# Three norm boundaries of a two-layer diffusion step: modulation sums in quarters, and three moves around them

## The chip, the cores and the metric

The kernel runs on one core of a Trainium2 chip. The core has a matrix engine (PE, in the profile; PEld is its weight load), a vector engine (DVE), a scalar engine (ACT), a general engine (POOL) and a queue that issues transfers (SP). The metric is the device time of one execution in microseconds; less is better.

## The reference, cut to what matters

Two groups of 128 tokens, a context pass and a denoising step, run through the same two layers with 2048 features. Each layer is a mixer (layer 0: latent attention and grouped attention side by side; layer 1: differential attention) and a gated convolutional FFN. Ahead of each of the four stands a norm with a modulation that comes from a condition vector:

```python
mod = jax.nn.silu(cond) @ w_ada[l] + b_ada[l]
sh1, sc1, gt1, sh2, sc2, gt2 = jnp.split(mod[:, None, :], 6, axis=-1)
h = rmsnorm(x, g_norm_mix[l]) * (1 + sc1) + sh1
...
x = x + gt1 * m
h = rmsnorm(x, g_norm_ffn[l]) * (1 + sc2) + sh2
x = x + gt2 * conv_ffn(h, ...)
```

So a norm needs all of x, a sum of squares over the features, and only then can the next weight product start. `w_ada` alone has 2 x 2048 x 12288 numbers, so its product is as much a matter of memory traffic as the layers are.

## The kernel before, in words

**Layout.** Everything is kept transposed: 128 partitions of features, 16 such chunks (KD = 16), 256 columns (NT: 128 tokens of each group). Float32 values are split into a high part (`wh`, `hx[:, k, :NT]`, a cast on ACT) and a low part (`wl`, `hx[:, k, NT:]`, a subtraction on DVE), and each product is three matmuls of 128 x 256: high-high, high-low, low-high. A weight chunk is 16 blocks of 128 x 128, loaded as one tile of 1 MB (`raw`), split in two halves of 8 blocks.

**Order.** A planner places instructions on each engine by a simulated time line, earlier ones first, so an instruction whose inputs are ready early may be placed ahead of others. `tc.keep_in_program_order(i)` (called `pin`) fixes an instruction behind the one that was traced just before it on its engine. `tc.issue_after(j)` places a block's instructions on j's engine behind j. On the chip each engine then works its own list in that order and waits by semaphores.

**The modulation.** `w_ada` is worked off in units (layer, which of the six vectors, quarter of its features). A unit of `ROWS` is four tiles of 1 MB in two buffers (`araw`). Tile t is summed by `sum_rows` (line 579) with four matmuls that go to four groups of 32 columns of the array, one for each quarter g of the tile; when all four tiles are in, `ada_finish` gives two steps: `copy` (line 523, ACT copies the sum out of PSUM into the tile `am`, of which there is one) and `turn` (line 530, four transposes on PE; then a reduction and an addition on DVE, lines 532 and 540). Most of these run through `row_step`, between the chunks of other products; `later` holds steps that are still to be taken. `ensure` takes steps until a unit is done. One unit is kept back for each boundary and summed inside `modulated`.

**A norm boundary.** There are three that go through `modulated`: A, from the output projection of layer 0's attention to the first FFN; B, from the first FFN to mixer C; C, from mixer C's output projection to the second FFN. At the last chunk (c = 15) of the stage before, `residual` first makes a `Ready`: it loads the next stage's first three weight chunks and splits four of their six halves ((0,0), (0,1), (1,0), (2,0)); the half (0,1) lies in a pool called `extra`. Then the residual is added (line 763, DVE), squared (line 191, ACT) and the squares are summed over the features by one-column matmuls with the running sum (line 229) and the last square (line 230). Then come a small scaling (line 206, DVE), the power -1/2 (line 210, POOL), a diagonal (line 236, DVE) and a matmul that spreads it over the partitions (line 244). In the gaps of this chain PE sums the first tile of the kept unit (ahead of the diagonal) and the second (behind line 244).

`rows_in_turn` then makes the 16 normed rows: for each, x times the spread factor (line 676, DVE), scale and shift for group 0 (line 692, DVE; rows 7 and 11 on ACT, line 690) and for group 1 (line 694, ACT), the cast into hx (line 695, ACT), and one row later the low part (line 679, DVE). Between rows stand the splits of the halves that are still open: `steps` names them by row. `Ready.product` (line 433) multiplies the three chunks with the rows as they come, 144 matmuls in the order `ORDER`, in which the third chunk runs two rows behind and the third modulation tile is summed at the place of `None`. The fourth tile's sum and the copy are handed on as `last_rows`, and the transposes as `turn`; they run in the middle of the next stage's fourth and fifth chunk (`between` in `gemm`).

**What follows the product.** `modulated` ends with `W.ahead(pin)`: the first half of the fourth chunk's weights is split (line 249 ACT, line 250 DVE), pinned. In an FFN stage the first three results go through `conv` with everything pinned: line 1355 (ACT), lines 1358 and 1361 (DVE), then another `W.ahead(pin)`. There are three PSUM banks for results (`acc`), so the fourth chunk's product waits until the first result has been read. In mixer C the first results are rotated and copied (lines 1247 to 1253), unpinned.

**Boundary A** has one thing more. Layer 0's unit (0, 3, 1) is still open when the last chunk of the output projection comes up; `ensure(l, 4)`, `ensure(l, 3)` and the loop over `later` trace its last sums, its copy and its transposes there, ahead of the chunk in the program's order but not pinned against it.

## Time and profile before

| | us |
|---|---|
| median of 3 runs (lowest, highest) | 2308.39 (2308.24, 2310.5) |
| the profiled execution, its own time | 2307.44 |
| its span, first to last instruction | 2305.7 |
| PE busy in the span | 2269.9 (98%) |
| DVE busy | 1824.0 (79%) |
| ACT busy | 1180.7 (51%) |
| HBM traffic | 603.01 MB read, 4.75 MB written |

Times in the trace count from the first instruction. A row of a timeline reads: start, duration, engine, line of the kernel, operation, out<-in, shape, count, and in brackets the idle time of the engine before it and what ended it. Matmuls are pipelined: one of 128 x 256 is listed with 0.28 us, while the next starts 0.11 us later. A row of the windows view reads: from:to, length, then busy time (and instructions) of PE, PEld, DVE, ACT and POOL, the granted clock of PE as a share of full speed, the share of the DMA engines' time, and GB/s.

### The profile page before, as it was taken

To read this page: it belongs to the slowest core of one execution; us is meant where nothing else is said; L and a number is where in the kernel's file an instruction comes from. 1 tells how busy PE (TensorE), PEld (TensorE's weight loads), DVE (VectorE), ACT (ScalarE), POOL (GpSimd) and SP (SyncE) were. 2 spreads that over 40 slices of the span, in tenths; PEclk is the share of its full clock that TensorE was granted. 3 is DMA by queue.
4 is the path that set the end of the run, shared out by engine and by line. 5 is a ranking of instruction groups with operands and counts; after the bars stand their busy time and mean duration, and the time that the engine had idled before them with its cause. 6 is when DMAs were issued, how large, how long until landed. Compare 5 with 4: busy or idle time off the path is not lost. (4 is left out here: it accounts for less than half of the span.)

```text
span 2305.7 us, 47396 instructions
## 1 busy us (share of the span) xinstructions
PE 2269.9 (98%) x19812; PEld 2178.4 (94%) x19812; DVE 1824.0 (79%) x2683; ACT 1180.7 (51%) x1880; POOL 117.4 (5%) x100
## 2 busy tenths in 40 slices
PE   8999999999999999999999999999999999999998
PEld 6888878799999999999989999898999999999997
DVE  5667749789989999999879989787899755666654
ACT  4347654655553455554465555446555434555553
POOL 0001101000000000002200000020000000000011
PEclk9999999999999999999999999999999999999999
DMA  9997789767768767777767787876677555555553
GB/s 390 386 368 276 298 325 393 261 233 263 257 248 311 291 260 272 254 260 273 291 238 271 294 316 288 313 297 236 241 256 262 193 199 188 199 191 193 200 188 125
DMA packets 92565, 610.81 MB, mean 265 GB/s; under 512 B 9984, under 2 KB 17856, under 8 KB 20544
## 3 DMA queue, kind: packets, MB, share of 16 engines
q1 hardware_dynamic: 92352, 607.80, 71.1%
q8 instruction: 155, 2.54, 0.4%
q14 instruction: 58, 0.48, 0.1%
HBM read 603.01 MB, written 4.75 MB: 264 GB/s over the span
## 5 line engine op out<-in xcount | busy, mean ns | idle before, releaser
L249 ACT CAST wh<-raw 128x1024 fp32r<-128x1024 f32 (+1 forms) x772 | 773.5, 1009 | 901.1 <-PE acc L447 685.7
L250 DVE TENSOR_TENSOR wl<-raw,wh 128x1024 fp32r<-128x1024 f32 (+1 forms) x772 | 899.8, 1182 | 286.2 <-ACT wh L249 278.5
L446 PE MATMUL acc<-hx,wh 128*128 128x256 f32 x3440 | 952.8, 277 | 2.3 <-DVE cv L1361 0.8
L450 PE MATMUL acc<-hx,wl 128*128 128x256 f32 x3440 | 951.4, 277 | 0.2 <-DVE wl L250 0.2
L447 PE MATMUL acc<-hx,wh 128*128 128x256 f32 x3440 | 951.5, 277 | 0.0
L446 PEld LDWEIGHTS acc<-hx,wh 128*128 128x128 f32 x3440 | 646.1, 188 | 9.9 <-issue 5.9
L450 PEld LDWEIGHTS acc<-hx,wl 128*128 128x128 f32 x3440 | 645.5, 188 | 6.4 <-issue 2.5
L447 PEld LDWEIGHTS acc<-hx,wh 128*128 128x128 f32 x3440 | 646.1, 188 | 1.0 <-issue 0.8
L556 DVE CUSTOM_DVE_ANT_0 junk<-araw,condb 128x2048 f32<-128x2048 f32 (+1 forms) x192 | 442.8, 2306 | 0.1
L447 PE MATMUL acc<-g,wh 128*128 128x256 f32 x1408 | 388.3, 276 | 0.0
L450 PE MATMUL acc<-g,wl 128*128 128x256 f32 x1408 | 388.0, 276 | 0.0
L446 PE MATMUL acc<-g,wh 128*128 128x256 f32 x1408 | 387.8, 276 | 0.0
L447 PEld LDWEIGHTS acc<-g,wh 128*128 128x128 f32 x1408 | 264.3, 188 | 0.0
L450 PEld LDWEIGHTS acc<-g,wl 128*128 128x128 f32 x1408 | 264.2, 188 | 0.0
L446 PEld LDWEIGHTS acc<-g,wh 128*128 128x128 f32 x1408 | 264.1, 188 | 0.0
L198 POOL TENSOR_TENSOR sqacc<-sqacc,sq 128x256 f32<-128x256 f32 x61 | 83.5, 1368 | 1607.7 <-issue 1250.8
L1013 PE MATMUL acc<-hx,wh 128*128 128x256 f32 x608 | 111.8, 284 | 1.0 <-ACT hx L983 0.6
L1013 PEld LDWEIGHTS acc<-hx,wh 128*128 128x128 f32 x608 | 92.7, 189 | 9.4 <-issue 4.9
L1355 ACT ACTIVATE cv<-acc,convw 128x256 f32<-128x256 f32 x176 | 98.4, 559 | 1.6 <-PE acc L433 1.6
L763 DVE SCALAR_TENSOR_TENSOR x<-acc,mod,x 128x128 f32<-128x128 f32 x192 | 57.9, 343 | 38.4 <-PE acc L450 37.5
L1361 DVE SCALAR_TENSOR_TENSOR cv<-acc,convw,cv 128x254 f32<-128x254 f32 x176 | 84.3, 479 | 3.7
L1013 PE MATMUL acc<-hx,wl 128*128 128x256 f32 x304 | 84.5, 279 | 0.0
(287 smaller groups left out, 2461.7 us busy)
## 6 DMA issues: line engine op xcount, KB each, us to landing
raw<-w_up SPq DMA_DIRECT2D x176, 1024.0 KB, 4.8
araw<-w_ada SPq DMA_DIRECT2D x160, 1024.0 KB, 5.3
raw<-w_down SPq DMA_DIRECT2D x88, 1024.0 KB, 4.8
raw<-w_in_c SPq DMA_DIRECT2D x48, 1024.0 KB, 5.6
raw<-w_in_ab SPq DMA_DIRECT2D x20, 1024.0 KB, 12.4
araw<-w_first SPq DMA_DIRECT2D x16, 1024.0 KB, 8.3
condb<-w_first SPq DMA_DIRECT2D x16, 1024.0 KB, 9.4
raw<-w_out_ab SPq DMA_DIRECT2D x16, 1024.0 KB, 6.9
```

The lines of the kernel that those rows point to most:

```text
L198: pool.tensor_tensor(out=st["acc"], in0=st["acc"], in1=sq, op=ALU.add)
L249: pin(act.copy(out_hi, src))
L250: pin(dve.tensor_tensor(out=out_lo, in0=src, in1=out_hi.bitcast(F32), op=ALU.subtract))
L446: fixed(pe.matmul(ps[:, :n], wh, xh(k), start=(i == 0), stop=False))
L447: fixed(pe.matmul(ps[:, :n], wh, xl(k), start=False, stop=False))
L450: fixed(pe.matmul(ps[:, :n], wl, xh(k), start=False, stop=(i == last)))
L556: tc.keep_in_program_order(dve.tensor_tensor_reduce(out=junk, in0=raw, in1=condb[:, c].rearrange("p (g n) -> p g n", g=4), scale=1.0, scal ...
L763: i = dve.scalar_tensor_tensor(out=x[:, c, s], in0=ps[:, s], scalar=mod[:, l, 3 * which + 2, c, g:g + 1], in1=x[:, c, s], op0=ALU.mult, op ...
L1013: pin(pe.matmul(ps, w, hx[:, k, lo:lo + NT], start=first and k == ks[0] and n == 0, stop=last and k == ks[-1] and n == 2, skip_group_check ...
L1355: pin(act.activation(y, ps, AF.Identity, scale=cw[:, 1, m:m + 1], bias=cw[:, 3, m:m + 1]))
L1361: pin(dve.scalar_tensor_tensor(out=y3[:, :, :T - 1], in0=p3[:, :, 1:], scalar=cw[:, 2, m:m + 1], in1=y3[:, :, :T - 1], op0=ALU.mult, op1=A ...
```

## The change

It has four parts, all at the norm boundaries.

1. *Quarters.* In `modulated` the kept unit's tiles are no longer summed one by one. `fill(n)` takes the next n quarters: three behind the old stage's last matmul, ahead of the statistic's matmuls (two at A); then, behind them, up to the end of tile 1 (at B three); then, behind the spreading matmul, the rest. All are pinned.
2. *Third tile, and third chunk's half, in old memory.* Where `more` is true (A and C, not B), the pool `extra` also takes the half (2,1) of the weights and three quarters of the unit's third tile (`next3`); its fourth quarter goes into the tile `am`. So the third tile's four quarters are summed behind the spreading matmul too, the cast of (2,1) moves from row 8 to the chain (behind that of (1,1)), and its low parts to rows 4 and 9. The product then takes the three chunks in step (`AT_ONCE`), with no sum inside. At B, `ORDER` and its sum stay.
3. *The end of the product.* At all three boundaries the fourth tile's sum is pinned directly behind the product and its copy follows, both ahead of `W.ahead(pin)`; only the transposes are left for the fourth chunk.
4. *Last visit ahead of the last chunk.* At A, unit (0, 3, 1) is summed and copied ahead of the last chunk, whose first matmul is pinned behind it (`held`); its transposes, reduction and addition run at the start of `modulated`, on DVE behind the last residual.

And the first row changes its order: row 1's product on DVE comes behind row 0's scaling, ACT writes row 0 into hx in two parts, and writes group 1 once more into h for the low part.

```diff
+AT_ONCE = [(c, k, part) for k in range(EARLY) for part in ("xl", "x") for c in (0, 1, 2)]
+AT_ONCE += [(c, k, "all") for k in range(EARLY, KD - 2) for c in (0, 1, 2)]
+AT_ONCE += [(c, k, "all") for c, k in ((0, KD - 2), (1, KD - 2), (0, KD - 1), (2, KD - 2), (1, KD - 1), (2, KD - 1))]
...
-        def __init__(self, W, extra):
+        def __init__(self, W, extra, more):
+            self.more = more
+            self.hi, self.lo = {}, {}
+            if more:
+                self.room(2, 1, extra)
+                self.third = T_(extra, [P, 3, 512], "next3", bufs=1)
             self.raws = [W.load() for _ in range(3)]
...
-    def gemm(blocks, xh, xl, n=NT, first=0, between=None):
-        fixed = lambda i: tc.keep_in_program_order(i) if between else i
+    def gemm(blocks, xh, xl, n=NT, first=0, between=None, held=False):
+        fixed = lambda i: tc.keep_in_program_order(i) if between or held else i
...
             fixed(pe.matmul(ps[:, :n], wh, xh(k), start=(i == 0), stop=False))
+            held = False
...
-            if c + 1 < KD:
+            if 0 < c < KD - 1:
                 times(c + 1)
...
+            if c == 0:
+                times(1)
+                pin(act.activation(hx[:, c, T:NT], h[:, T:], AF.Identity, scale=a_(1), bias=b_(1)))
+                pin(act.copy(hx[:, c, :T], h[:, :T]))
             pin(act.activation(h[:, T:], h[:, T:], AF.Identity, scale=a_(1), bias=b_(1)))
-            pin(act.copy(hx[:, c, :NT], h))
             if c:
+                pin(act.copy(hx[:, c, :NT], h))
                 low(c - 1)
...
+        turn = later.pop() if (l, which) == (0, 1) and len(later) == 1 else None
+        if turn:
+            done.add((0, 3, 1))
...
+        if ready.more:
+            parts = ready.third, T_(tmp, [P, 512], "am", bufs=1)
+            for part, g in zip(parts, (slice(0, 3), 3)):
+                sp.dma_start(out=part, in_=A["w_ada"][u[0], u[1], u[2], 2][:, g])
+        groups = [raws[t][:, g] for t in range(2) for g in range(4)]
+        if ready.more:
+            groups += [parts[0][:, 0], parts[0][:, 1], parts[0][:, 2], parts[1]]
         hx = T_(keep, [P, KD, ROW], "hx", F32R)
+        ada["ps"] = bank()
+        at = [0]
+
+        def fill(n):
+            for _ in range(n):
+                t, g = divmod(at[0], 4)
+                pin(pe.matmul(ada["ps"][32 * g:32 * g + 32, :], condw[:, 4 * t + g, :], groups[at[0]],
+                              start=(t == 0), stop=(t == 3), skip_group_check=True))
+                at[0] += 1
+
         tied[0] = True
+        if turn:
+            with tc.issue_after(st["added"]):
+                turn()
+        fill(2 if turn else 3)
         ready.room(1, 1)
         with tc.issue_after(st["squared"]):
             ready.high(1, 1)
+            if ready.more:
+                ready.high(2, 1, pin=pin)
         r = stat_rstd(st, D, att_bank)
-        sum_rows(0, raws[0], bank())
+        fill(8 - at[0] if ready.more else 3)
         dg = diagonal(r, (0, 1))
         ready.low(1, 1, 0, 4, pin)
         rb = spread(dg, bank=att_bank)
-        sum_rows(1, raws[1])
+        fill(len(groups) - at[0])
         tied[0] = False
-        raws += [load_tile(2), load_tile(3)]
+        rest = range(at[0] // 4, 4)
+        raws = {t: load_tile(t) for t in rest}
...
+        low = lambda c, a: lambda: ready.low(c, 1, a, a + 4, pin)
+        rows_in_turn(hx, rb, l, which, {4: low(2, 0), 8: low(1, 4), 9: low(2, 4)} if ready.more else
+                     {5: low(1, 4), 8: second, 10: low(2, 0), 12: low(2, 4)})
         ada["i"] += 1
-        rest = ada_finish(*u)
-
-        def last_rows():
-            sum_rows(3, raws[3])
-            rest[0]()
-
-        def turn():
-            rest[1](pin)
-
-        ps = ready.product(hx, lambda: sum_rows(2, raws[2]))
+        last = ada_finish(*u)
+        ps = ready.product(hx, AT_ONCE if ready.more else ORDER, lambda: sum_rows(2, raws[2]))
+        sum_rows(3, raws[3], pin=pin)
+        last[0]()
         W.ahead(pin)
-        return hx, ps, [last_rows, turn]
+        return hx, ps, [lambda: last[1](pin)]
...
                 if c == KD - 1:
-                    ensure(l, 4)
-                    ensure(l, 3)
-                    while later:
+                    while ada["i"] <= ROWS.index((l, 3, 1)):
+                        row_step()
+                    while len(later) > 1:
                         later.pop(0)()
-                residual(gemm(W.chunk(), oh, ol, first=8), l, 0, c, st, lambda: (then, feat["pool"]))
+                residual(gemm(W.chunk(), oh, ol, first=8, held=c == KD - 1), l, 0, c, st,
+                         lambda: (then, feat["pool"], True))
```

At C the pool is `cx`, also with `True`; at B it is the FFN's own, with `False`.

More of the change, by code (lines that the diff above doesn't have):

```diff
@@ L417, in block, with product @@
             return self.hi[c, h][:, s], self.lo[c, h][:, s]
-        def product(self, hx, mid):
+        def product(self, hx, order, mid):
             pin = tc.keep_in_program_order
@@ L423, in product @@
             left = [3 * KD] * 3
-            for item in ORDER:
+            for item in order:
                 if item is None:
@@ L573, in feature_step, with sum_rows @@
             feat["t"] = 0
-    def sum_rows(t, raw, ps=None):
+    def sum_rows(t, raw, ps=None, pin=None):
         if t == 0:
@@ L580, in sum_rows @@
                           start=(t == 0), stop=(t == 3), skip_group_check=True)
-            if pinned[0]:
+            if pinned[0] or pin:
                 tc.keep_in_program_order(i)
@@ L1331, in mixer_c @@
                 fine[0] = c >= KD - QUIET[2]
-                residual(ready.pop(0) if ready else gemm(W.chunk(), oh, ol), l, 0, c, st, lambda: (then, cx))
+                residual(ready.pop(0) if ready else gemm(W.chunk(), oh, ol), l, 0, c, st, lambda: (then, cx, True))
                 pump(RATE["outc"] if c < KD - QUIET[2] else 0)
@@ L1385, in room @@
                 T_(fp, [P, 16], "pad2", bufs=1)
-                return then, fp
+                return then, fp, False
             def down(gs, q):
```

6 lines of the change are left out of this document (1 added, 5 removed).

## The prediction

> **What bounds the kernel now.** I read the page first (its head and part 1), then the windows view with the granted clock, then the timelines of PE, DVE and ACT around the three norm boundaries: A, attention output into the first FFN, near 420 us; B, first FFN into mixer C, near 1155 us; C, mixer C output into the second FFN, near 1565 us.
>
> ```profile
> span 2305.7 us, 47396 instructions
> PE 2269.9 (98%) x19812; PEld 2178.4 (94%) x19812; DVE 1824.0 (79%) x2683; ACT 1180.7 (51%) x1880; POOL 117.4 (5%) x100
> ...
> 470.00:1050.00 580.00, 580.00 (x5120) 580.00 (x5119) 532.50 (x673) 289.97 (x380) 0.00 (x0) 1.00 0.72 265
> ...
> 419.96:423.38 3.42, 1.91 (x16) 0.74 (x14) 0.73 (x3) 1.53 (x2) 0.00 (x0) 1.00 1.01 393
> 423.38:426.79 3.41, 1.82 (x14) 0.90 (x14) 1.52 (x5) 1.44 (x3) 0.71 (x1) 1.00 0.66 267
> ...
> 1153.83:1157.24 3.41, 2.49 (x20) 1.23 (x21) 1.41 (x5) 1.44 (x3) 0.71 (x1) 1.00 0.12 20
> ...
> 1563.43:1566.84 3.41, 2.23 (x19) 1.23 (x17) 1.19 (x6) 1.44 (x3) 0.71 (x1) 1.00 0.00 0
> 1566.84:1570.25 3.41, 3.29 (x11) 0.98 (x12) 2.70 (x9) 1.40 (x4) 0.00 (x0) 0.50 0.78 274
> ```
>
> PE bounds the kernel: it is busy 580 of 580 us between boundaries, so whatever a boundary gains or loses reaches the end unchanged. At the boundaries PE runs short of work, and after C's thin window (2.23 us busy, a good part of it one-column products) the clock is granted at 0.50 for the next 3.41 us. B's window with 2.49 us busy keeps 1.00. Here is B, undisturbed, then C:
>
> ```profile
> 1153.07 0.28 PE L450 MATMUL acc<-g,wl 128*128 128x256 f32 x1
> ...
> 1154.19 0.38 PE L230 MATMUL att<-cst,sq 128*128 128x1 f32 x2 [0.73 <-ACT sq L191]
> ...
> 1156.58 0.70 PE L244 MATMUL att<-diag,cst 128*128 128x256 f32 x2 [0.56 <-DVE diag L236]
> ...
> 1158.87 0.39 PE L433 MATMUL acc<-hx,wh 128*128 128x256 f32 x1 [0.60 <-ACT hx L695]
> ...
> 1157.32 0.75 DVE L676 TENSOR_TENSOR nt<-x,att 128x256 f32<-128x256 f32 x2 [0.19 <-PE att L244]
> ```
>
> ```profile
> 1563.45 0.28 PE L450 MATMUL acc<-oall,wl 128*128 128x256 f32 x1
> ...
> 1565.33 1.06 PE L579 MATMUL misc<-araw,condw 128*32 128x512 f32 x8
> 1566.96 1.22 PE L244 MATMUL att<-diag,cst 128*128 128x256 f32 x2 [0.56 <-DVE diag L236]
> ...
> 1568.22 0.75 DVE L676 TENSOR_TENSOR nt<-x,att 128x256 f32<-128x256 f32 x2 [0.71 <-PE att L244]
> ```
>
> From the last old matmul (call its start E) to the first row product on DVE (L676, call it R) B takes 1157.32 - 1153.07 = 4.25 us and C, with L244 at half clock, 4.77. A has a delay of its own ahead of the chain:
>
> ```profile
> 419.82 0.28 PE L450 MATMUL acc<-hx,wl 128*128 128x256 f32 x1
> ...
> 420.14 1.06 PE L579 MATMUL ada<-araw,condw 128*32 128x512 f32 x8
> 421.92 0.66 PE L530 MATMUL ada<-cst,am 128*128 128x128 f32 x4 [0.71 <-ACT am L523]
> ...
> 421.28 0.59 ACT L523 COPY am<-ada 128x512 f32<-128x512 f32 x1 [3.51 <-PE ada L579]
> 421.76 1.05 ACT L407 CAST wh<-raw 128x1024 fp32r<-128x1024 f32 x1
> ...
> 422.92 1.22 DVE L410 TENSOR_TENSOR wl<-raw,wh 128x1024 fp32r<-128x1024 f32 x1
> 424.06 0.60 DVE L763 SCALAR_TENSOR_TENSOR x<-acc,mod,x 128x128 f32<-128x128 f32 x2
> ...
> 428.50 0.75 DVE L676 TENSOR_TENSOR nt<-x,att 128x256 f32<-128x256 f32 x2 [0.71 <-PE att L244]
> ```
>
> The last visit's sum (L579) runs after the last chunk. The copy of it (L523) keeps ACT waiting 3.51 us, a weight cast and its low part queue behind the copy, and the residual L763 behind that: it starts 4.2 us after E, where it could start 0.3 after (the matmul's own 0.28). R comes at 428.50, 8.68 us after E. The reader should keep the pair L523, L407 in mind: ACT works its queue in order, and a cast traced behind that copy waits for the copy's sum.
>
> **The change, boundary by boundary.** *A, last visit ahead of the last chunk.* The sum tile (1.06 us) now delays the last chunk: E = 419.82 + 1.06 = 420.88. The residual follows E at once, if the third chunk's cast and low part are done by then; their tile is no longer behind the copy, and I cost this at nothing (ends: 0, or 1.2 for one more L410 behind it). Transposes (0.66 as a lone group, about 0.5 in a stream) and two quarters of a sum now stand ahead of the statistic's matmuls. Four quarters take 1.06 together; two or three run side by side on other columns, so I take the same 1 us. The gap that they fill is about 1 us (0.73 idle before L230 in B, and the first L229 pair's share), so three quarters alone push L230 by 0.3, and with transposes by 0.8. The six quarters of the next gap use two column groups twice, some 1.9 us against 1565.33 to 1566.96 = 1.63: 0.2 more. R = 420.88 + 4.25 + 0.8 + 0.2 = 426.1, a gain of 2.4.
>
> *C.* Three quarters (+0.3) and five (+0.2) on 4.25: R = E + 4.75, against 4.77 now. The filled gaps remove the half clock (0.5) and cost the same.
>
> *B.* Three quarters in each gap, two behind: +0.3, nothing gained.
>
> *The product.* In A and C the third tile leaves the product (one sum tile, 1.06), the casts of chunk three's second half leave the rows for the gap, and the three chunks go in step. What limits is DVE's rows:
>
> ```profile
> 1570.10 0.41 DVE L676 TENSOR_TENSOR nt<-x,att 128x256 f32<-128x256 f32 x1
> ...
> 1570.68 0.42 DVE L679 TENSOR_TENSOR hx<-nt,hx 128x256 fp32r<-128x256 f32 x1
> 1571.02 0.41 DVE L676 TENSOR_TENSOR nt<-x,att 128x256 f32<-128x256 f32 x1
> ...
> 1573.80 0.68 DVE L410 TENSOR_TENSOR wl<-raw,wh 128x512 fp32r<-128x512 f32 x1
> 1574.40 0.40 DVE L676 TENSOR_TENSOR nt<-x,att 128x256 f32<-128x256 f32 x1
> ```
>
> A row costs 0.92 on DVE, a weight half-piece 0.60. The low part of row 9 stands behind 0.9 of start, ten rows and all three pieces (steps 4, 8, 9), less 0.26 for row 7 scaled on ACT: R + 0.9 + 9.2 + 1.8 - 0.26, about 11.8, with short waits on ACT 12.1. Behind it PE has 62 matmuls at 580 / 5120 = 0.113 us: 7.0. So the product ends near R + 19.2. Now it ends at R + 20.46 (1568.22 to 1588.57 + 0.11, rows below): 1.25 less in A and C. Bounds: 0, where DVE limits as now, to 2.6, where only the 144 matmuls (16.3) and B's start (1157.32 to 1158.87, 1.55) count. That row 0 comes out sooner is worth nothing, since row 9 decides. B keeps its order. Sum up to here: A -2.4 - 1.25 = -3.65, B +0.3, C -1.25: **-4.6 us**.
>
> *Behind the product.* This part decides the sign. The fourth tile's sum and its copy move from inside the fourth chunk to right behind the product, **ahead of `W.ahead(pin)`**. That call pins its cast behind whatever was traced last on ACT, and that is now the copy L523, which waits for a sum that is pinned behind the whole product. In both FFN stages the first convolution's L1355, L1358 and L1361 are pinned behind that cast and its low part, and the fourth chunk needs the bank that L1361 frees:
>
> ```profile
> 1585.69 1.05 ACT L249 CAST wh<-raw 128x1024 fp32r<-128x1024 f32 x1
> 1587.53 0.57 ACT L1355 ACTIVATE cv<-acc,convw 128x256 f32<-128x256 f32 x1 [0.79 <-PE acc L433]
> ...
> 1586.77 1.23 DVE L250 TENSOR_TENSOR wl<-raw,wh 128x1024 fp32r<-128x1024 f32 x1 [0.53 <-ACT wh L249]
> 1588.13 0.48 DVE L1358 SCALAR_TENSOR_TENSOR cv<-acc,convw,cv 128x254 f32<-128x254 f32 x1
> 1588.65 0.48 DVE L1361 SCALAR_TENSOR_TENSOR cv<-acc,convw,cv 128x254 f32<-128x254 f32 x1
> ...
> 1588.57 0.28 PE L433 MATMUL acc<-hx,wl 128*128 128x256 f32 x1
> 1589.27 0.36 PE L446 MATMUL acc<-hx,wh 128*128 128x256 f32 x1 [0.42 <-DVE cv L1361]
> ...
> 1177.69 0.28 PE L433 MATMUL acc<-hx,wl 128*128 128x256 f32 x1
> ...
> 1178.76 0.38 PE L446 MATMUL acc<-hx,wh 128*128 128x256 f32 x1 [0.67 <-DVE dq L1251]
> ```
>
> Now the cast starts 2.9 us before the last product matmul (P = 1588.57) and the fourth chunk 0.70 after it. Afterwards: sum done at P + 1.25, copy at 1.32, cast at 1.81 (421.28 to 421.76 is 0.48), low part 2.9, L1358 4.03 (L410 to L763 above: 1.14), L1361 4.55, its end 5.03, fourth chunk 5.17. PE loses 5.17 - 0.70 = 4.47 and gets back 1.05, the sum that no longer interrupts the fourth chunk: **+3.4 in A and in C**. Bounds: a gain of 0.6, where the copy doesn't hold the cast and the sum fills the hole of 0.7; 4.5, where the moved sum saves nothing. In B nothing but the cast is pinned, so banks come free as now, but the fourth chunk's first low part is there at P + 4.15 against 1.41 now (0.34 behind its first matmul at 1.07): 2.74 - 1.05 = **+1.7** (ends -0.8 and 3).
>
> *The clock.* PE is then idle for 3.9 us (A, C) and some 2.6 (B), and the rows above show half clock after a window with far more work. Wherever the 3.41 us grid falls on 3.9 us of idle, one window has under 1.6 us of work; the next lies 1.3 to 3.4 us on busy PE and loses about half: 0.65 to 1.7, I take 1.3 each. B: three quarters of the phases, 1.0. Sum +3.6 (ends 0 and 5).
>
> The Trainium skill says otherwise on the last point ("TensorE: Matmul & The Clock Gate", section "What's actually happening"): half rate comes after at least one idle window of about 3.4 us. Taken literally, 3.9 us of idle hold a whole window in one phase of seven, and the sum below would be about 4.3 in place of 7.5. The trace disagrees: 1563.43 to 1566.84 held 2.23 us of work and was followed by 0.50.
>
> Other edits cost nothing: the third tile's transfer replaces one issued behind the chain, and SP's queue can issue it as soon as its new memory is free; in A the quarter that goes into the "am" tile waits for the transposes, but the product has about 1.8 us of slack at its start, since row 9 decides (if more is late: up to 2). Chunk three's cast in the gap finds ACT idle before R.
>
> **Sum.** -4.6 + 3.4 + 3.4 + 1.7 + 3.6 = **+7.5 us**. The profiled execution took 2307.44 (span 2305.7 and 1.7 around it), so it gives 2314.9; the median of the runs, 2308.39, lies 0.95 above that execution, and I carry that on: **2315.9 us**.
>
> **Rivals.**
> 1. *The copy doesn't hold the cast* (faster). It decides by one place: whether L523 stands ahead of L249 in ACT's order behind the rows. If not, the sum fills the hole: -4.6 - 0.6 - 0.6 - 0.8 = -6.6, no half clock: 2301.8. For it: the copy itself is unpinned, and in A now three casts run ahead of one. Against: those were traced with other casts between; here the pin names the copy.
> 2. *Stalls without half clock.* 7.5 - 3.6 = +3.9, 2312.3. For it: the window at 419.96 with 1.91 us busy was followed by 1.00. Against: the row at 1563.43. The Trainium skill's rule, above, points this way too.
> 3. *A's gain fails*: quarters wait for late tiles, or the planner leaves the visit behind the last chunk and nothing is changed there. +3 to 3.65 more: 2319.2. Against: the slot for the second tile comes free with the earlier sum.
>
> **Chances.** Forecast 0.58 (its own range 2313.2 to 2318.5), rival 1 0.16, rival 2 0.16, rival 3 0.10. A measurement can tell about 0.2%, that is 2303.8 and 2313.0. Faster: rival 1, 0.15. Slower: the forecast, rival 3, and a fifth of rival 2, 0.69. Same: the rest, 0.16. The range 2310 to 2319.5 leaves out rival 1 and a little above.
>
> **What would show it.** ACT's row for L523 with several us of idle before it, ended by PE misc L579, then L249, at all three boundaries; the first L446 of each stage some 4 to 5 us behind the last L433; windows with 0.50 right behind; in A, L763 within 0.5 us of the last L450, and no 0.50 between L230 and L433. If L446 follows the last L433 within 1.5 us, the step behind the product was wrong and the time is near 2302.

## The result, and the profile after

The changed kernel takes 2320.95 us (median of 4 runs, 2319.94 to 2322.45) against 2309.23 us (2308.24 to 2310.5) for the kernel before: ratio 1.0051, 95% interval 1.0034 to 1.0068. It is slower, by 11.7 us at the medians. The forecast was 2315.9 with a range of 2310 to 2319.5: the sign was right, the size too small, and the time lies above the range. The profiled execution of the changed kernel took 2321.82 (span 2320.0), the one of before 2307.44 (span 2305.7), so between the two traces 14.3 us have to be found. One run of the kernel e3 below (2544.15) had a mean granted clock of 0.85 and is left out of its times.

From the page of the changed kernel, its head, part 1, and the group of the first matmul of each weight block (L453, which was L446), with its idle time and what ended most of it at the right:

```profile
span 2320.0 us, 47387 instructions
PE 2277.0 (98%) x19812; PEld 2182.8 (94%) x19812; DVE 1823.8 (79%) x2683; ACT 1180.5 (51%) x1881; POOL 118.7 (5%) x100
...
L453 PE MATMUL acc<-hx,wh 128*128 128x256 f32 x3440 | 954.5, 278 | 10.1 <-DVE cv L1395 7.8
```

Two idle times of 3.9 us stand in that last number. Here they are in the timeline of PE, at A and at C: the last product matmul (start P), the moved sum (L587), the fourth chunk's first matmul:

```profile
448.79 0.28 PE L440 MATMUL acc<-hx,next2wl 128*128 128x256 f32 x1
448.99 1.06 PE L587 MATMUL misc<-araw,condw 128*32 128x512 f32 x8
453.97 0.55 PE L453 MATMUL acc<-hx,wh 128*128 128x256 f32 x1 [3.91 <-DVE cv L1395]
...
1597.45 0.28 PE L440 MATMUL acc<-hx,next2wl 128*128 128x256 f32 x1
...
1602.64 0.44 PE L453 MATMUL acc<-hx,wh 128*128 128x256 f32 x1 [3.91 <-DVE cv L1395]
```

The fourth chunk starts at P + 5.18 and P + 5.19. The timelines of ACT and then DVE behind A's product show why: ACT waits 3.70 us for the sum, copies it (L531), and only then casts (L252); the low part, and the first convolution's steps L1389, L1392, L1395, follow in the order in which they were pinned.

```profile
450.12 0.58 ACT L531 COPY am<-misc 128x512 f32<-128x512 f32 x1 [3.70 <-PE misc L587]
450.61 1.05 ACT L252 CAST wh<-raw 128x1024 fp32r<-128x1024 f32 x1
451.55 0.57 ACT L1389 ACTIVATE cv<-acc,convw 128x256 f32<-128x256 f32 x1
...
452.83 0.47 DVE L1392 SCALAR_TENSOR_TENSOR cv<-acc,convw,cv 128x254 f32<-128x254 f32 x1
453.34 0.48 DVE L1395 SCALAR_TENSOR_TENSOR cv<-acc,convw,cv 128x254 f32<-128x254 f32 x1
```

At B the copy holds the cast too. The first matmul of the fourth chunk waits 1.34 us for the cast and its third one 0.76 for the low part, which is there at P + 4.18 (P is 1183.66, 0.21 ahead of the sum as at A):

```profile
1183.87 1.07 PE L587 MATMUL misc<-araw,condw 128*32 128x512 f32 x8
1186.58 0.39 PE L453 MATMUL acc<-hx,wh 128*128 128x256 f32 x1 [1.34 <-ACT wh L252]
1187.84 0.39 PE L458 MATMUL acc<-hx,wl 128*128 128x256 f32 x1 [0.76 <-DVE wl L253]
```

The windows view gives the price in clock (columns: us, busy time and instructions of PE, PEld, DVE, ACT and POOL, granted clock, DMA share, GB/s). At A three windows are at half clock, one ahead of the product and two behind it; at C one. The first line is of the kernel before, which has one at A too, about its spreading matmul.

```profile
426.79:430.20 3.41, 2.96 (x10) 0.70 (x10) 2.69 (x9) 1.09 (x3) 0.00 (x0) 0.50 0.66 231
...
421.75:425.17 3.42, 2.16 (x15) 1.07 (x13) 2.01 (x5) 1.81 (x4) 0.00 (x0) 1.00 1.00 412
425.17:428.58 3.41, 3.41 (x14) 0.75 (x14) 1.24 (x4) 1.40 (x2) 0.71 (x1) 0.50 0.53 180
...
449.05:452.47 3.42, 1.01 (x9) 0.10 (x8) 0.78 (x1) 2.35 (x4) 0.00 (x0) 1.00 0.35 86
452.47:455.88 3.41, 1.91 (x9) 1.94 (x10) 3.34 (x7) 3.38 (x5) 0.00 (x0) 0.50 0.53 223
455.88:459.30 3.42, 3.42 (x18) 3.42 (x18) 2.87 (x6) 2.15 (x5) 0.00 (x0) 0.50 0.84 307
...
1599.35:1602.77 3.42, 0.13 (x1) 0.16 (x2) 2.38 (x4) 3.42 (x6) 0.00 (x0) 1.00 0.88 285
1602.77:1606.18 3.41, 3.41 (x17) 3.41 (x18) 3.20 (x5) 2.21 (x4) 0.00 (x0) 0.50 0.39 137
```

What stands behind the product was in the forecast, but for the second window at A. What was not is A's side ahead of the product. PE's timeline: two tiles of the last visit, then the last chunk, whose first matmul waits 0.90 for a cast and whose third one waits 0.58 for a low part of *its own* weights; its last matmul (E) starts at 421.28.

```profile
412.15 1.92 PE L587 MATMUL ada<-araw,condw 128*32 128x512 f32 x16
414.98 0.39 PE L453 MATMUL acc<-hx,wh 128*128 128x256 f32 x1 [0.90 <-ACT wh L252]
416.06 0.38 PE L458 MATMUL acc<-hx,wl 128*128 128x256 f32 x1 [0.58 <-DVE wl L253]
...
421.28 0.28 PE L458 MATMUL acc<-hx,wl 128*128 128x256 f32 x1
```

ACT, then DVE, around it. The last chunk's casts (L252) stand behind the square of the chunk before (L200), for which ACT idles 5.18 us. The residual (L796) starts at 423.75, 2.47 behind E, behind a low part (L417) of the third FFN chunk that waited for its cast (L414). The first row product (L684, R) comes at 429.53:

```profile
412.96 0.42 ACT L200 ACTIVATE sq<-x 128x256 f32<-128x256 f32 x1 [5.18 <-DVE mod L548]
413.29 2.16 ACT L252 CAST wh<-raw 128x512 fp32r<-128x512 f32 x4
...
421.52 1.05 ACT L414 CAST wh<-raw 128x1024 fp32r<-128x1024 f32 x1 [2.74 <-PE acc L455]
```

```profile
413.92 2.69 DVE L253 TENSOR_TENSOR wl<-raw,wh 128x512 fp32r<-128x512 f32 x4 [0.98 <-ACT wh L252]
...
422.60 1.22 DVE L417 TENSOR_TENSOR wl<-raw,wh 128x1024 fp32r<-128x1024 f32 x1 [2.56 <-ACT wh L414]
423.75 0.60 DVE L796 SCALAR_TENSOR_TENSOR x<-acc,mod,x 128x128 f32<-128x128 f32 x2
...
429.53 0.42 DVE L684 TENSOR_TENSOR nt<-x,att 128x256 f32<-128x256 f32 x1 [1.97 <-PE att L247]
```

In the kernel before, the last chunk's casts ran ahead of that square (L197 there), and its low parts were done at 413.80, 2.8 us earlier than here (416.61):

```profile
407.94 1.14 ACT L249 CAST wh<-raw 128x512 fp32r<-128x512 f32 x2 [1.53 <-PE acc L447]
...
414.50 0.42 ACT L197 ACTIVATE sq<-x 128x256 f32<-128x256 f32 x1 [5.10 <-DVE x L763]
...
410.78 3.02 DVE L250 TENSOR_TENSOR wl<-raw,wh 128x512 fp32r<-128x512 f32 x4
```

One more place is late in this execution, in the attention of mixer C, far from every edit: PE waits for a copy (L839) that stands on ACT behind a cast, and that cast waits for a weight transfer which took 7.4 us from issue to landing, where the same transfer took 5.2 in the trace of before.

```profile
1466.41 1.04 ACT L252 CAST wh<-raw 128x1024 fp32r<-128x1024 f32 x1 [1.85 <-DMA raw<-w_out_c]
...
1467.89 0.70 PE L1328 MATMUL att<-dv,pT 128*128 128x256 f32 x2 [1.41 <-ACT pT L839]
```

With E, R, P and the start of the fourth chunk (called F) read off the two timelines, the 14.3 us are found. "End" is the start of the fourth chunk's last matmul; clock is half of the busy time in the 0.50 windows behind the product; the sum tile that no longer interrupts the fourth chunk is 1.05.

| term, us | forecast | traces |
|---|---|---|
| A: E, 419.82 to 421.28 | +1.06 | +1.46 |
| A: E to R, 8.68 to 8.25 | -3.46 | -0.43 |
| A: R to P, 20.36 to 19.26 | -1.25 | -1.10 |
| A: P to F, 0.70 to 5.18, less 1.05 | +3.4 | +3.43 |
| A: clock behind the product, (1.91 + 3.42) / 2 | +1.3 | +2.7 |
| B, from A's end to B's (from +6.06 to +8.00) | +3.0 | +1.9 |
| mixer C, from B's end to C's E | 0 | +1.7 |
| C: E to R, R to P (20.36 to 19.51) | -1.25 | -0.9 |
| C: P to F, 0.70 to 5.19, less 1.05 | +3.4 | +3.44 |
| C: clock, 3.41 / 2 | +1.3 | +1.7 |
| behind C, and rounding | 0 | +0.4 |
| sum | +7.5 | +14.3 |

### The profile page after: what moved, and what is told of

Its sections match the earlier page's. It is cut to its first block, busy times and chain, and to the rows that moved or that the text cites. A ratio compares the mean times of both kernels' runs of the same rounds, so it can differ in the third digit from the quotient of the medians.

```text
span 2320.0 us, 47387 instructions
## 1 busy us (share of the span) xinstructions
PE 2277.0 (98%) x19812; PEld 2182.8 (94%) x19812; DVE 1823.8 (79%) x2683; ACT 1180.5 (51%) x1881; POOL 118.7 (5%) x100
## 4 chain that ended last, share of the span: by engine, by line
PE 90%; DVE 4%; DMA 3%; ACT 1%; issue 1%; SPq 0%; POOL 0%; DVEq 0%; POOLq 0%; ACTq 0%
PE acc L458 25%; PE acc L453 25%; PE acc L455 25%; PE acc L1046 3%; PE ada L587 2%; PE acc L369 1%; PE acc L370 1%; PE acc L372 1%; DVE wl L253 1%; PE ada L492 1%; PE acc L440 1%; DMA araw<-w_ada 1%; DMA raw<-w_in_ab 1%; PE att L1046 1%; DMA araw<-w_first 1%
## 5 line engine op out<-in xcount | busy, mean ns | idle before, releaser
L252 ACT CAST wh<-raw 128x1024 fp32r<-128x1024 f32 (+1 forms) x772 | 773.3, 1010 | 895.8 <-PE acc L455 675.7
L253 DVE TENSOR_TENSOR wl<-raw,wh 128x1024 fp32r<-128x1024 f32 (+1 forms) x772 | 899.5, 1182 | 308.3 <-ACT wh L252 300.4
L453 PE MATMUL acc<-hx,wh 128*128 128x256 f32 x3440 | 954.5, 278 | 10.1 <-DVE cv L1395 7.8
L455 PE MATMUL acc<-hx,wh 128*128 128x256 f32 x3440 | 953.0, 277 | 0.0
L453 PEld LDWEIGHTS acc<-hx,wh 128*128 128x128 f32 x3440 | 648.0, 188 | 17.3 <-ACT cv L1389 9.6
L455 PEld LDWEIGHTS acc<-hx,wh 128*128 128x128 f32 x3440 | 648.1, 188 | 0.2
L455 PE MATMUL acc<-g,wh 128*128 128x256 f32 x1408 | 388.3, 276 | 0.0
L453 PE MATMUL acc<-g,wh 128*128 128x256 f32 x1408 | 387.8, 276 | 0.0
L455 PEld LDWEIGHTS acc<-g,wh 128*128 128x128 f32 x1408 | 264.3, 188 | 0.0
L453 PEld LDWEIGHTS acc<-g,wh 128*128 128x128 f32 x1408 | 264.1, 188 | 0.0
L1389 ACT ACTIVATE cv<-acc,convw 128x256 f32<-128x256 f32 x176 | 98.2, 558 | 0.0
L1395 DVE SCALAR_TENSOR_TENSOR cv<-acc,convw,cv 128x254 f32<-128x254 f32 x176 | 84.4, 480 | 3.8
L796 DVE SCALAR_TENSOR_TENSOR x<-acc,mod,x 128x128 f32<-128x128 f32 x192 | 57.9, 343 | 35.1 <-PE acc L458 34.1
```

The lines of the kernel that those rows point to most:

```text
L252: pin(act.copy(out_hi, src))
L253: pin(dve.tensor_tensor(out=out_lo, in0=src, in1=out_hi.bitcast(F32), op=ALU.subtract))
L453: fixed(pe.matmul(ps[:, :n], wh, xh(k), start=(i == 0), stop=False))
L455: fixed(pe.matmul(ps[:, :n], wh, xl(k), start=False, stop=False))
L796: i = dve.scalar_tensor_tensor(out=x[:, c, s], in0=ps[:, s], scalar=mod[:, l, 3 * which + 2, c, g:g + 1], in1=x[:, c, s], op0=ALU.mult, op ...
L1389: pin(act.activation(y, ps, AF.Identity, scale=cw[:, 1, m:m + 1], bias=cw[:, 3, m:m + 1]))
```

## The experiments

**What holds the fourth chunk.** Three kernels. The first moves one call of the changed kernel:

```
 ps = ready.product(hx, AT_ONCE if ready.more else ORDER, ...)
+W.ahead(pin)
 sum_rows(3, raws[3], pin=pin)
 last[0]()
-W.ahead(pin)
```

> The changed kernel with one call moved: W.ahead(pin) is traced ahead of the fourth tile's sum and its copy, so the cast no longer stands behind the copy. The copy still stands directly behind the cast on ACT, ahead of the first convolution L1389. Theory 1 (ACT's order behind the copy sets the fourth chunk): cast back at 3 us before the last product matmul P, but L1389 still waits for the copy; copy done P + 1.81, L1389, L1392, L1395 0.5 each, fourth chunk at P + 3.4 in A and C in place of 5.18; in B the first low part is there on time again. A -1.8, C -1.8, B -1.7, so about 2315.5, and less if the half-clock windows behind the product go. Theory 2 (the cast alone is the holder): fourth chunk at P + 1.25 at once, some 13 us less, 2308. Theory 3 (something else, the accumulator banks or the weights' transfer, sets it): P + 5.2 as before, 2321.

Measured: 2314.46 us median against 2309.52 on the same chip, ratio 1.0043 (1.0007 to 1.0080); the changed kernel stood at 1.0051. ACT, then PE, of this kernel at A (P is 449.62):

```profile
450.96 0.59 ACT L531 COPY am<-misc 128x512 f32<-128x512 f32 x1 [2.75 <-PE misc L587]
451.44 0.57 ACT L1389 ACTIVATE cv<-acc,convw 128x256 f32<-128x256 f32 x1
...
453.19 0.36 PE L453 MATMUL acc<-hx,wh 128*128 128x256 f32 x1 [2.30 <-DVE cv L1395]
```

The fourth chunk starts at P + 3.57 (at C 3.57 too), not 5.18 and not 1.25. The cast is out of the way and the copy still holds L1389: theory 1. What ACT holds behind the copy is the convolution as much as the cast.

The second takes the copy out of the way altogether, into the middle of the fourth chunk:

```
 sum_rows(3, raws[3], pin=pin)
-last[0]()
 W.ahead(pin)
-return hx, ps, [lambda: last[1](pin)]
+return hx, ps, [last[0], lambda: last[1](pin)]
```

(`W.ahead` stays behind the sum, other than the expectation says; the sum is PE's, so ACT's order is the same.)

> The changed kernel with W.ahead(pin) traced first and the copy of the fourth tile's sum moved into the middle of the fourth chunk (the sum itself stays pinned behind the product). Theory 1 (ACT's order behind the copy): fourth chunk at P + 1.25 in A and C, right behind the sum, no idle of PE and no half clock behind the product: A -3.9 - 2.3, C -3.9 - 1.3, B -1.7: 13 less, about 2308. What is left against the kernel before is then the loss ahead of A's product (the last chunk waits for its weights, the residual 2.5 us behind it), some 4.7, against 1.1 won in each of two products. Theory 2 (the loss behind the product is only half of it, and the idle comes back as a wait for weights or banks): 2314 or more.

Measured: 2308.57, ratio 0.9998 (0.9989 to 1.0008) to the kernel before, so all of the loss is gone with two lines. No window behind a product is at half clock. The chunk starts at P + 2.06, not P + 1.25:

```profile
448.25 0.56 ACT L1389 ACTIVATE cv<-acc,convw 128x256 f32<-128x256 f32 x1 [1.72 <-PE acc L440]
...
449.99 0.36 PE L453 MATMUL acc<-hx,wh 128*128 128x256 f32 x1 [0.79 <-DVE cv L1395]
```

The convolution waits for the product itself here (P is 447.94), and the fourth chunk comes 1.74 us after it starts. In the kernel before (at C), the first of the three chunks starts its last matmul at P - 1.36 and the convolution follows at P - 1.04; here that matmul is at P - 1.02 and the convolution at P + 0.31. So PE stands still 0.79 us although the sum now lies in the hole, where it stood still 0.42 before. From R to the fourth chunk's end it is 26.74 us at A (27.79 before): the product's gain survives.

The third puts the end of the product alone into the kernel before:

```
-def last_rows(): sum_rows(3, raws[3]); rest[0]()
 ps = ready.product(hx, lambda: sum_rows(2, raws[2]))
+sum_rows(3, raws[3], pin=pin)
+rest[0]()
 W.ahead(pin)
-return hx, ps, [last_rows, turn]
+return hx, ps, [lambda: rest[1](pin)]
```

> The kernel before with one part of the change alone: the fourth tile's sum, pinned, and its copy right behind the product and ahead of W.ahead(pin), at all three boundaries. Theory as recorded: fourth chunk at P + 5.2 in A and C in place of 0.70, less 1.05 for the sum, +3.4 each; B +1.7; half clock behind it 1.3 to 2.4 in A and C: +11 to +12, about 2321. Rival (the stall needs the changed order of the product, which ends 1.1 sooner): fourth chunk at P + 4 or less, +7, 2316.

Measured: 2320.37, 2350.32 and 2352.48, ratio 1.0127 (1.0077 to 1.0177). The last of these, the one with a trace, holds something else, shown in the last section, so the ratio doesn't price the edit; the shortest is 10.5 above the 2309.90 of before, near what was expected. ACT and PE at A:

```profile
453.57 0.58 ACT L523 COPY am<-misc 128x512 f32<-128x512 f32 x1 [4.13 <-PE misc L579]
454.05 1.05 ACT L249 CAST wh<-raw 128x1024 fp32r<-128x1024 f32 x1
...
457.41 0.55 PE L446 MATMUL acc<-hx,wh 128*128 128x256 f32 x1 [3.91 <-DVE cv L1356]
```

P + 5.18 at A and at C, within a hundredth of what the whole change has, with the old order of the product: the rival is out.

**What the clock costs.** Matmuls of the modulation's form fill PE's hole behind A's and C's product, and leave ACT and DVE as they are:

```
 sum_rows(3, raws[3], pin=pin)
+if ready.more:
+    spare = att_bank()
+    for i in range(36):                 # 18 in the second kernel
+        g = i % 4
+        pin(pe.matmul(spare[32 * g:32 * g + 32, :], condw[:, 12 + g, :], raws[3][:, g],
+                      start=True, stop=True, skip_group_check=True))
 last[0]()
```

> The changed kernel with 36 more one-third-empty matmuls of the modulation's form (condw against the fourth tile) pinned behind the fourth tile's sum in A and C, into a bank that nobody reads: they fill PE's idle 3.9 us and leave the copy, the cast and the fourth chunk where they are (P + 5.2). Only the clock is changed. Theory 1 (idle time of PE lowers the clock of the next 3.41 us window, and that costs PE's time): no 0.50 behind the product; A gets back 2.3, C 1.3, about 2317.3. The window with 0.50 ahead of A's product stays. Theory 2 (the half clock costs nothing, since weights are late there anyway): 2321. Theory 3 (these thin matmuls don't count as work for the clock, as one-column ones did not seem to): 0.50 stays, 2321.

Measured: 2338.87 (4 runs, from 2324.68), ratio 1.0152 (1.0081 to 1.0224). The time says nothing of the clock: each call is two instructions, 36 of them take 7.91 us, and the fourth chunk starts at P + 8.93. A failed experiment as a time; but no window behind the two products is at 0.50. Half as many fit the hole:

> As the run with 36 matmuls in the idle time (they took 7.9 us, twice the hole), with 18: they end at P + 5.1, so the fourth chunk starts at P + 5.2 to 5.3 as in the changed kernel and only the clock differs. Theory 1: no 0.50 in the windows behind the product of A and C, fourth chunk 6.0 us from its first to its last first-pass matmul in place of 8.4 (A) and 7.5 (C): 3.9 us less than the changed kernel. Theory 2 (the half clock is hidden by late weights): 8.4 and 7.5 stay.

Measured: 2318.09 (5 runs), ratio 1.0029 (1.0017 to 1.0042); F at P + 5.48, 0.3 later than in the changed kernel, and the stretch where that kernel had two windows at half clock now reads:

```profile
452.50:455.90 3.40, 3.40 (x32) 0.79 (x21) 2.57 (x4) 3.40 (x5) 0.00 (x0) 1.00 0.01 2
455.90:459.30 3.40, 3.40 (x31) 3.40 (x30) 3.00 (x5) 2.19 (x5) 0.00 (x0) 1.00 0.65 214
```

From its first matmul to its end (as in the table) the fourth chunk takes 6.01 us at A and at C, where the changed kernel takes 8.38 and 7.48. ACT's and DVE's order is the same in both, so the half clock cost 2.4 and 1.5 us: theory 1. (The total gains 3.5 by the two differences to the kernel before, 8.2 and 11.7, after the 0.3 lost at each start.)

**What delays A ahead of its product.** First the one part that was to win there, alone in the kernel before:

```
 if c == KD - 1:
-    ensure(l, 4)
-    ensure(l, 3)
-    while later:
+    while ada["i"] <= ROWS.index((l, 3, 1)):
+        row_step()
+    while len(later) > 1:
         later.pop(0)()
...
+if turn:
+    with tc.issue_after(st["added"]):
+        turn()
```

> The kernel before with one part of the change alone: the last visit's sums ahead of the last chunk of the attention output, its transposes behind the last residual; quarters, third tile, order and the end of the product as before. Theory as recorded: last chunk 1.06 later, residual at once behind it, first row product 2.4 us earlier, -2.4: 2306.8. Theory from the changed kernel's trace: the last chunk waits for its own weights (1.6 more), and the residual stands behind the third chunk's cast, whose buffer comes free only with the last chunk's last matmul, and its low part (2.2): first row product 1 to 2.3 us later than before, 2310 to 2311.5.

Measured: 2307.40, ratio 0.9996 (0.9986 to 1.0005): no change that these runs can tell, though 2.4 us (0.9990) lies inside the interval. The trace decides, and for neither theory. DVE's first row product, then PE:

```profile
425.93 0.75 DVE L677 TENSOR_TENSOR nt<-x,att 128x256 f32<-128x256 f32 x2 [0.19 <-PE att L244]
...
427.99 1.93 PE L580 MATMUL misc<-araw,condw 128*32 128x512 f32 x8 [2.10 <-DMA araw<-w_ada]
```

R comes 4.25 us behind E and 2.57 before that of the kernel before (428.50): the recorded 2.4 is really won (3.4, counted from the end of the chunk before, and E comes the forecast 1.06 later by that count). But the second tile's sum is pinned ahead of the product, its tile lands 2.1 us after PE is ready for it, and from R to P it is 22.84 in place of 20.36. The gain goes into a transfer. In this kernel the residual isn't late; so what delays it in the changed kernel isn't the visit alone.

Then three kernels on f1's base. The profile names PE's L455 as what ended the third chunk's cast; that is the buffer of the last chunk's first eight blocks, which it multiplies last. Taking the blocks in order frees that buffer earlier:

```
-gemm(W.chunk(), oh, ol, first=8, ...)
+gemm(W.chunk(), oh, ol, first=8 if c < KD - 1 else 0, ...)
```

> As f1, and the last attention-output chunk takes its sixteen blocks in their order instead of from the ninth on, so that the buffer of its first eight blocks, which the third FFN chunk's cast takes over, is free 2.7 us before E and not at E. Theory 2 (the cast waits for that buffer, as the profile's row names the releaser): E to the first row product 7.1 -> about 5. Theory 1 (it waits for its raw weights, which land at that time): 7.1 stays, or more, since the last chunk's low parts of the first blocks come no sooner.

Measured (one run, 2308.27): the cast starts 9.58 us behind the last matmul of the chunk before, exactly as in f1, though the buffer is free earlier. (E to R is 9.43; this execution has a half-clock window at 424.50, f1 has none.) ACT's row now names another releaser:

```profile
420.85 1.04 ACT L414 CAST wh<-raw 128x1024 fp32r<-128x1024 f32 x1 [2.73 <-DMA raw<-w_up]
```

The cast waits for its raw weights, and theory 2 is out. In the changed kernel SP issues that transfer at 416.63, as the last chunk's last low part (L253, 413.92 + 2.69 = 416.61) lets go of a raw buffer; it lands 4.8 us later, at 421.43 (here the two transfers of that stretch), and the cast starts at 421.52, 0.10 behind. The same 0.10 stands between that landing and the cast in the traces of e1, f1, e2, e2b, e4, f4, f2, f6 and f7:

```profile
L270 SPq DMA_DIRECT2D raw<-w_up x2: 328/328/328, 416.6 to 418.9; - x2
...
DMA to landing us min/median/max: 4.8/5.1/5.5
```

So one place is late, the last chunk's own split, and the last chunk, the transfer, the cast, the low part and the residual are late behind it. Casting it earlier:

```
 blocks = ahead.pop(0) if ahead else W.chunk()
+if c == KD - 2:
+    ahead.append(W.chunk(tc.keep_in_program_order))
+st["pin"] = c == KD - 2       # the square of this chunk's residual is pinned behind it
```

> As the run with the copy in the middle of the fourth chunk (f1), and beside it the last attention-output chunk's weights are cast and split ahead of the residual of the chunk before it, pinned there on ACT and DVE. In the changed kernel that cast stands on ACT behind the square of that residual. Theory 1 (this one place makes all of A's loss ahead of the product: the last chunk waits for its low parts, and the raw buffer that they free late delays the transfer of the third FFN chunk's weights, whose cast and low part stand ahead of the residual): last chunk 1.5 earlier, and from the last matmul E to the first row product 4.3 to 5.2 us in place of 7.1; 3.5 to 4 us less than f1, about 2305. Theory 2 (the third chunk's cast waits for its own buffer, freed with the last chunk's last matmul): E 1.5 earlier, E to the first row product 7.1 as before, 2307.

Measured: 2307.76, ratio 0.9999 (0.9980 to 1.0019); E to R 6.64 in place of 7.13: between the two theories, and the expected 3.5 to 4 us did not come. The casts moved from 413.6 to 407.3, but the low parts still stand behind two feature sums on DVE and end at 415.53, 1.3 earlier than in f1, half of which is this execution's lead (the square of the third chunk from the end starts at 407.00, in f1 at 407.62). So, on top of that, the third chunk's low part was taken from ahead of the residual:

```
-self.low(c, h, pin=...)                      # (2, 0), ahead of the residual
...
 r = stat_rstd(st, D, att_bank)
...
+if ready.late: ready.low(2, 0, 0, 4, pin)
 dg = diagonal(r, (0, 1))
+if ready.late: ready.low(2, 0, 4, 8, pin)
```

> As f2 (copy in the middle of the fourth chunk, last attention-output chunk's weights split early), and in A the low part of the third FFN chunk's first half, which stood on DVE ahead of the last residual, is traced behind the statistic, in two halves of 0.6 us beside the diagonal. Theory 1, mended (the raw tile of the third chunk is issued when the last chunk's last low part frees its buffer and lands 4.8 us later; cast and low part follow, and the residual stands behind them): residual at once behind E, its square behind the cast that still waits for the transfer; E to the first row product 6.64 -> 5.1 to 5.5, 1.3 us less than f2. Theory 3 (the chain from residual to row product is itself longer in A, because of transposes and quarters): 6.6 stays.

Measured: **2306.10, ratio 0.9982 (0.9973 to 0.9992) to the kernel before: faster than both kernels.** DVE:

```profile
421.09 0.61 DVE L803 SCALAR_TENSOR_TENSOR x<-acc,mod,x 128x128 f32<-128x128 f32 x2 [1.58 <-PE acc L461]
...
426.46 0.42 DVE L687 TENSOR_TENSOR nt<-x,att 128x256 f32<-128x256 f32 x1
```

The residual waits for the chunk's matmul alone (0.32 behind E at 420.77), and R comes 5.69 behind E: theory 1, with 0.2 to 0.6 more than expected, and theory 3 is out.

**What is left.** The visit put back behind the last chunk, on f1's base:

```
 if c == KD - 1:
-    while ada["i"] <= ROWS.index((l, 3, 1)):
-        row_step()
-    while len(later) > 1:
+    ensure(l, 4)
+    ensure(l, 3)
+    while later:
         later.pop(0)()
...                                            # and `held` goes
```

> As f1, with the last visit of the attention output put back behind the last chunk, as before the change: what is left of the change is quarters, third tile and order. Theory as recorded (they win 1.1 to 1.25 in the product of A and C, and cost 0.3 to 0.8 ahead of it): A from E to the first row product 8.7 to 9.4, first row product to P 19.3 in A and C, whole kernel 1 to 2 us under before but for what the transfers of mixer C cost. Rival (the visit is worth its recorded 2.4 once the stall is gone): f5 2.4 slower than f1. From f1's trace (E to the first row product 7.1, with the last chunk 1.5 late): f5 within 0.5 of f1.

Measured: 2308.93, ratio 0.9994 (0.9985 to 1.0004), 0.4 from f1's 2308.57. That doesn't make the visit's place worth nothing. From the end of the chunk before (412.82; in f1 412.21) R is 2.0 us later than in f1: the visit's last sum falls into the last chunk, at 422.62, and one window at half clock, at 417.90, into the same place. Mixer C's stretch, which varies (next section), is 2.0 shorter than in f1's trace and hides it. The last chunk's cast stands behind the square of the chunk before in this kernel as well (it starts at 414.17), while in the kernel with the visit alone it ran at 408.74. So the late split comes with the other parts of the change (the third tile and half chunk in old memory, the quarters); by which of them the written order of ACT turned was not tried.

Last, on top of f6, chunk one was made to end sooner, to free its bank:

```
-((0, KD-2), (1, KD-2), (0, KD-1), (2, KD-2), (1, KD-1), (2, KD-1))
+((0, KD-3), (1, KD-3), (0, KD-2), (0, KD-1), (1, KD-2), (2, KD-3), (1, KD-1), (2, KD-2), (2, KD-1))
```

> As f6, and in the order by which A and C go through three chunks in step, the last nine entries are turned so that the first chunk ends 15 matmuls (1.7 us) ahead of P in place of 9 (1.0). In f1 the fourth chunk waits 0.79 us behind the sum for the bank that the first chunk's convolution frees, and that begins when the first chunk's last matmul is done. Theory 1: fourth chunk at P + 1.4 in place of 2.06 in A and C, about 1.2 us less than f6. Rival: the first chunk then waits for the last rows (they end about 1.9 us before P) and P comes later by as much: no change.

Measured: 2305.22, ratio 0.9993 (0.9965 to 1.0022); F stays at P + 2.06. P doesn't come later either, so the rival's reason is not it: the convolution starts at P + 0.3 although chunk one's last matmul starts at P - 1.77.

```profile
449.14 0.56 ACT L1401 ACTIVATE cv<-acc,convw 128x256 f32<-128x256 f32 x1 [1.97 <-PE acc L443]
```

Why it waits for the whole product stays open. The sum pinned behind the product is not the reason: at B, in f1's trace, the same sum stands there with the old order, and the first copy out of a bank comes at P - 1.02 (1176.32 against 1177.34).

## Why the prediction was right or wrong

*Behind the product: right, to the hundredth.* Forecast P + 5.17 at A and C, measured 5.18 and 5.19; at B the first low part at P + 4.15, measured 4.18. The working (sum, copy, cast, low part, two convolution steps, bank) is what the rows show, step for step, and e1, f1 and e3 show the cause: take the copy from ahead of the cast and the convolution, and the loss goes; put it there in the kernel before, and it comes. Rival 1 is out.

*The clock: right in kind, short in size.* 1.3 each was forecast for A and C; the fill kernel prices it at 2.4 and 1.5. I averaged over the places at which the 3.41 us grid can fall, for one window; at A a boundary splits the hole of 3.9 us in 2.4 and 1.5, and it costs two, 452.47 and 455.88; at C one window holds 3.3 of it, and it costs one. (e3 has it the other way round: one at A, where one window holds 3.3, and two at C, split in 2.6 and 1.3.) At B, where I took 1.0, this execution has none; two other kernels with the same stall there have one (e2 and e3, at 1190). Rival 2 is out at A and C, and at B it is what happened. It is the one towards which the Trainium skill's rule points ("TensorE: Matmul & The Clock Gate", section "What's actually happening": half rate after at least one idle window). The trace agrees at C, where the window at 1599.35 holds 0.13 us of work, and disagrees at A, where 421.75 holds 2.16 us and the next is at 0.50. How much work a window needs these traces don't tell: f1's at 421.50 holds 2.17 us and is followed by 1.00.

*The product: nearly right.* R to P was to be 19.1 (to the product's end 19.2); it is 19.26 at A and 19.51 at C. The low part of row 9 was to end at R + 12.1, ends at R + 12.17, and PE waits 0.20 for it, at A and at C. (The terms that the working writes down add up to 11.64, not 11.8.) What the step left out shows in f1: with this order the first convolution waits for the whole product, and the fourth chunk gets its bank only at P + 2.06. Under the stall of the copy this costs nothing, and without it 0.4.

*A ahead of the product: wrong, and this is the step that failed.* "The residual follows E at once, if the third chunk's cast and low part are done by then; their tile is no longer behind the copy, and I cost this at nothing (ends: 0, or 1.2 for one more L410 behind it)." The condition was named and not checked against the queue that feeds it. The last chunk's own cast had slipped behind a square on ACT, so its low parts, the third FFN chunk's transfer, cast and low part, and the residual all came late; the sign set down for it (the residual within 0.5 us of E) reads 2.47. E to R was to be 5.22 and is 8.25: the residual 2.2 late, and a half-clock window at 425.17 that slows the quarters and L247 by 1.1 more (8.16 and 8.19 in e1 and e2b, which have such a window; 7.13 and 7.14 in f1 and e2, which don't). E itself was to be 1.06 later and is 1.46 later in spite of an execution that stood about 1.2 ahead in the chunks before (the same matmuls, 408.19 there, 406.95 here), since the last chunk waits for its weights, 0.90 and 0.58. Together 3.4 us more than forecast by the table, and the lead hides another 1.2. Rival 3 named A's gain as what could fail and gave 2319.2, nearest of all; one of its two mechanisms, a late tile, is what eats the gain in e4, but in the changed kernel it is another, the late split.

*The rest of the gap.* Mixer C's 1.7 us were no term of the sum. f1 and f6 issue the same transfer at the same place in their order, and it takes 7.7 us in f1 and 5.0 in f6. From B's end to C's E six of the ten kernels with the quarters need 379.2 to 380.4 us and four 377.8 to 378.4; the three without (before, e3, e4) need 377.9 to 378.2. What makes the transfer longer, and whether the change makes that likelier, was not found. At the medians the change costs 11.7, not 14.3; the two profiled executions lie 1.8 below and 0.9 above theirs.

## What to carry to other kernels

Work that is put behind a stage to fill a hole brings its reader with it: look on the reader's engine for what stands behind it in order, since a copy that waits for the last matmul of a stage holds all casts and bank releases that stand behind it. When a wait is removed, follow what stood in its shadow back to its transfer and to the buffer that lets the transfer start; here low parts that ended 2.8 us later moved a transfer, a cast and a residual. A gap of PE should be costed with the next clock windows: here 3.9 us of it cost two of them where a boundary split it in 2.4 and 1.5, and one where one window held nearly all of it.

## What was not expected of the hardware

In the profiled execution of e3 the matmuls of the last FFN run at a lower rate with the clock granted in full: 852 in 100 us, where the kernel with the visit alone has 885 and no idle time in either. Over the stage that makes 27 us (736.8 from the end of C's fourth chunk, 709.9 in the changed kernel). The slower step is not e3's alone: in the changed kernel's mixer C, from 1466 to 1500, most matmuls are 0.117 or 0.118 us apart as in e3's stage, against 0.113 or 0.114 from 1505 on; new in e3 is that it lasts for a whole stage. What sets it was not found. Runs some 25 to 30 us above the others of their kernel stand in e1, e2, f2 and f7 too; none of them has a trace. Windows view, e3 and then the other:

```profile
1800.00:1900.00 100.00, 100.00 (x852) 100.00 (x851) 64.85 (x84) 44.01 (x53) 0.00 (x0) 1.00 0.53 187
```

```profile
1800.00:1900.00 100.00, 100.00 (x885) 100.00 (x884) 57.90 (x74) 41.59 (x44) 0.00 (x0) 1.00 0.54 193
```

And the name of a releaser can hide a second one where two waits end together: in the changed kernel PE's L455 ends at 421.44 and the transfer lands at 421.43, and the cast is put down to L455; in f4, where the buffer is free earlier, it is put down to the transfer and starts no sooner.
